# Low parts of weights by accumulating DMA instead of a subtraction on VectorE, in a two-layer decoder step

## The chip, the core and the metric

The kernel runs on one core of one Trainium2 chip. The metric is the device time of one execution, in microseconds (us). Two timed runs of the kernel before took 2398.39 and 2399.04 us, median 2398.72 us. One further execution was profiled; it took 2399.39 us, and its first and last instruction lie 2397.4 us apart (the span).

## The reference

The reference is one inference step of a small decoder with 512 prompt positions and 32 new tokens (8 sequences of 4), so 544 columns of activations, width 1024. Two layers follow each other, each a SwiGLU, a mixer and another SwiGLU:

```python
for i in range(DEPTH):                                        # DEPTH = 2
    xp = xp + 0.5 * swiglu(rmsnorm(xp, norm_ffn1[i]), w_ffn1_in[i], w_ffn1_out[i])
    hp = rmsnorm(xp, norm_mix[i])
    # even layer: dilated-window attention, q/k/v of 3 groups x 8 heads x 64, one output projection
    # odd layer:  chunked gated MLP, u, v = split(gelu(h W_uv)), v = layernorm(v), (u * (tril(W_s) v + b)) W_o
    xp = xp + mp
    xp = xp + 0.5 * swiglu(rmsnorm(xp, norm_ffn2[i]), w_ffn2_in[i], w_ffn2_out[i])

def swiglu(x, w_in, w_out):
    gate, up = jnp.split(x @ w_in, 2, axis=-1)                # 1024 -> 2 x 2816
    return (jax.nn.silu(gate) * up) @ w_out                   # 2816 -> 1024
```

The same is done for the 32 new tokens, with cached keys and values in the attention. Everything is float32: the weights come from HBM as float32, and the products have to hold that precision.

## The kernel before, in words

TensorE is fed 32-bit operands in a rounded format (F32R). To keep float32 precision, every operand is split into a high part (the value rounded) and a low part (the value less the high part), and each product is three matmuls: high weights times high activations, high weights times low activations, low weights times high activations (`passes`, one of each per 128 x 128 weight tile and 272 columns). A weight tile's parts are called `wh` and `wl`.

The work is a sequence of *mults*. Each takes one slab of raw weights, K feature tiles of 128 rows by 256 columns (K is 8, 6 or 2), that one DMA on SyncE's queue brings into one of three buffers `raw` (two during the attention). There are two ways to multiply:

- `plain` splits the slab into its two column halves (`split` once per half), and runs 4 output quarters x K tiles x 3 passes, which is 96 matmuls for K = 8 and 72 for K = 6. It serves the output projections, the attention's projections and the first gate of each feed-forward part.
- `seven` serves the other gate and up slabs and the gated MLP's u and v. It forms sums and differences of the slab's four quarters on VectorE (`s13`, `s24`) and does seven products in place of eight, 84 matmuls. It needs four splits: of the quarter `a11` (128 x 512), of `s13` and `s24` (128 x 1024), and last of the odd feature tiles of the slab as they are (128 x 1024), which give the weights of the products that `c11` and `c21` close.

`split` (lines 219 to 226) is one ScalarE copy that rounds into `wh`, and one VectorE subtraction that writes `wl`. Both go into one of `g.nw` = 4 pairs of buffers, so a split can start only when the matmuls that read the buffer's former content are through. The products land in PSUM banks; ScalarE copies three of a seven's out (`k1`, `k5`, `k6`), VectorE the others, and both also prepare the activations' high and low parts (`spread`).

The order on every engine is made by a scheduler when the program is built; it goes by its own estimate of how long each instruction takes, and interleaves the products of neighbouring mults on TensorE accordingly. Each engine then works off its list in that fixed order, whatever the times are on the chip. `g.soon()` raises the priority of a piece of work during the attention, while `g.few` is set.

GpSimd (POOL) has work only in the attention and, once, two multiplications and additions in the gated MLP.

Of the kernel before, what the change touches and what calls it, by code (L numbers as in the profile page):

```python
# [9 lines left out]
F32 = mybir.dt.float32  # L10
F32R = mybir.dt.float32r
AF = mybir.ActivationFunctionType
ALU = mybir.AluOpType
# [3 lines left out]
P = 128  # L17
D = 1024
KD = D // P
# [5 lines left out]
NEG = -1.0e30  # L25
RMS_EPS = 1e-6
LN_EPS = 1e-5
SCRATCH = 64
XC = 256

UNITS = "U0 AV' BV' b A0 K0 B0 U1 E0 rk0 K1 B1 U2 rk1 K2 A12 B2 U3 E12 rk2 M D v0 v1 U4 v2"
# [197 lines left out]
def split(g, a):  # L229

    k, n = a.shape[1:]
    t = [g.wp.tile([P, KD * P], F32R, tag=nm, name=nm, bufs=g.nw)[:, :k * n].rearrange("p (k n) -> p k n", k=k) for nm in ("wh", "wl")]
    g.nc.scalar.copy(t[0], a)  # L233
    add(g.nc.vector, t[1], a, t[0], ALU.subtract)
    return t
# [13 lines left out]


def load_raw(g, src, K, cols):
    raw = g.raw()[:, :K * cols].rearrange("p (k n) -> p k n", k=K)
    g.nc.sync.dma_start(raw, src.rearrange("(k p) n -> p k n", p=P))
    return raw


def plain(g, raw, K, x, ev, hook=None):

    ws = []
    for c in range(2):  # L260
        with g.soon():
            ws.append(split(g, raw[:, :K, c * P:(c + 1) * P]))
    w = lambda c, k: [v[:, k] for v in ws[c]]
    halves = [(c, h) for c in range(2) for h in range(2)]

    def take(c, h, z):
        with g.soon():
            ev.full(c, h, z)

    if hook is None:  # L270
        for c, h in halves:
            z = g.bank("z")[:, :H2]
            for k in range(K):
                passes(g, z, w(c, k), x.tile(k, h), k == 0, k == K - 1)
            take(c, h, z)
        return

    g.late()
    zs = [g.bank("z")[:, :H2] for _ in halves]
    for k in range(K - 2):  # L280
        for (c, h), z in zip(halves, zs):
            passes(g, z, w(c, k), x.tile(k, h), k == 0, False)
    hook()
    for (c, h), z in zip(halves, zs):
        for k in range(K - 2, K):
            passes(g, z, w(c, k), x.tile(k, h), False, k == K - 1)
        take(c, h, z)


def seven(g, raw, K, x, ev, hook=None):  # L290

    nc = g.nc
    n = K // 2
    rv = raw[:, :K].rearrange("p (k e) (i c) -> p e i k c", e=2, i=2)
    a11, a12, a21 = rv[:, 0, 0], rv[:, 1, 0], rv[:, 0, 1]
    a22 = rv[:, 1, 1]
    V = nc.vector
    s13, s24 = (g.wp.tile([P, 2, 4, P], F32, tag=f"s{i}", name=f"s{i}")[:, :, :n] for i in range(2))

    def parts(a):  # L300
        with g.soon():
            return split(g, a)

    def take(to, z):
        with g.soon():
            to(z)

    def both(s):
        v = parts(s.rearrange("p i k c -> p (i k) c"))
        return [u[:, :n] for u in v], [u[:, n:] for u in v]  # L310

    w1 = parts(a11)
    with g.soon():
        add(V, s13[:, 0], a21, a22, ALU.add)
        add(V, s13[:, 1], a11, a21, ALU.subtract)
    w5, w7 = both(s13)
    with g.soon():
        add(V, s24[:, 0], s13[:, 0], a11, ALU.subtract)
        add(V, s24[:, 1], a12, s24[:, 0], ALU.subtract)
    z1, z3, z2 = g.banks()  # L320
    product(g, z1, w1, x.b(B11), True, True)
    take(ev.p1, z1)
    product(g, z3, w5, x.t(T1), True, True)
    take(ev.p5, z3)
    w6, w3 = both(s24)
    product(g, z1, w6, x.t(T2), False, True)
    take(ev.p6, z1)
    product(g, z3, w3, x.b(B22), False, True)
    take(ev.c12, z3)
    v = parts(raw[:, :K].rearrange("p (k e) n -> p e k n", e=2)[:, 1])  # L330
    w2, w4 = ([u[:, :, i * P:(i + 1) * P] for u in v] for i in range(2))
    product(g, z1, w7, x.t(T3), False, True)
    take(ev.c22, z1)
    product(g, z2, w2, x.b(B21), True, True)
    take(ev.c11, z2)
    product(g, z1, w4, x.t(T4), False, True)
    take(ev.c21, z1)
# [360 lines left out]

def qkv_unit(g, w_qkv, units, dst, hook):

    raw = g.raw().rearrange("p (k n) -> p k n", k=KD)
    for e, (c, gi, hp) in enumerate(units):
        col = ((c * 3 + gi) * 8 + 2 * hp) * 64
        g.nc.sync.dma_start(raw[:, :, e * P:(e + 1) * P], w_qkv[:, col:col + P].rearrange("(k p) n -> p k n", p=P))
    mult(g, "qkv", raw, KD, g.xop, Rows(g, dst, [u[1] > 0 for u in units], hook is not None), hook)


# [469 lines left out]
def gmlp(g, xop, w_uv, ln_g, ln_b, w_s, b_s, w_out, v_out, nxt):  # L1177
    nc = g.nc
    vd = g.tc.nc.dram_tensor("v_rows", (T, DV), F32, kind="Internal").ap()
    with ExitStack() as stack:  # L1180
# [10 lines left out]
        def spatial():  # L1191
            wn = gp.tile([P, 4 * H2], F32, tag="abl1", name="wsn")[:, :8 * P].rearrange("p (k s) -> p k s", k=8)
            nc.scalar.dma_start(wn, w_s.rearrange("g t s -> t g s"))
            nc.vector.tensor_tensor(wn, wn, cst[:, C_TRIL - C_B:C_TRIL - C_B + 128].unsqueeze(1).to_broadcast([P, 8, P]), op=ALU.mult)
            for gq in range(2):
                ps = g.bank("sm")
                for k in range(4):
                    nc.tensor.transpose(ps[:, k * P:(k + 1) * P], wn[:, 4 * gq + k], g.ident)
                nc.vector.tensor_copy(wst[:, 4 * gq:4 * gq + 4], ps.rearrange("p (k t) -> p k t", k=4))
            ps = g.bank("sm")  # L1200
            ws4 = gp2.tile([4, 8, 4], F32, tag="ws4", name="ws4")
            nc.vector.tensor_copy(ws4, wst[:4, :, :4])
            nc.tensor.matmul(ps[:32, :32], cst[:4, C_REP - C_B:C_REP - C_B + 32], ws4.rearrange("p g t -> p (g t)"), start=True, stop=True)
            ws32 = gp2.tile([32, 8, 4], F32, tag="ws32", name="ws32")
            nc.vector.tensor_copy(ws32, ps[:32, :32].rearrange("p (g t) -> p g t", g=8))
            for k in range(8):
                nc.vector.tensor_tensor(wss[:, k], ws32[:, k].unsqueeze(1).to_broadcast([32, 8, 4]),
                                        cst[:32, C_BM - C_B:C_BM - C_B + 32].rearrange("p (b t) -> p b t", t=4), op=ALU.mult)
# [84 lines left out]
        def mixing(j, vn, vs):  # L1293

            for n in range(4):
                nc.scalar.activation(vn[:, n], vn[:, n], AF.Identity, bias=lt[:, n:n + 1], scale=lr[:, n:n + 1])
            nc.scalar.activation(vs, vs, AF.Identity, bias=lt[:32, 4:5], scale=lr[:32, 4:5])
            mix = g.pair()
            for i in range(2):
                gq = (j + i) // 3  # L1300
                iss = slice(i * P, (i + 1) * P)
                if gq not in rows:
                    rsb = gp2.tile([P, P], F32, tag="rsb", name="rsb")
                    bsb = gp2.tile([P, P], F32, tag="bsb", name="bsb")
                    nc.scalar.dma_start(bsb, b_s[gq:gq + 1].to_broadcast([P, P]))
                    pr = g.bank("sm")
                    nc.tensor.matmul(pr[:, :P], g.cst[:, C_ONES:C_ONES + 128], wst[:, gq], start=True, stop=True)
                    nc.scalar.activation(rsb, pr[:, :P], AF.Copy, scale=float(D))
                    rows[gq] = rsb, bsb
                pm = g.bank("sm")  # L1310
                for n in range(4):
                    nc.tensor.matmul(pm[:, n * P:(n + 1) * P], vn[:, n, iss], wst[:, gq], start=True, stop=True)  # L1312
                pn = g.bank("sm")
                nc.tensor.matmul(pn[:, :32], vs[:, iss], wss[:, gq].rearrange("p b t -> p (b t)"), start=True, stop=True)
                rsb, bsb = rows[gq]
                gc = g.gT[:, 48 + j + i:49 + j + i]
                bc = g.gT[:, 72 + j + i:73 + j + i]
                off = gp.tile([P, P], F32, tag="off", name="off")
                nc.vector.scalar_tensor_tensor(off, rsb, bc, bsb, op0=ALU.mult, op1=ALU.add)
                fo = mix[:, i]  # L1320
                nc.vector.scalar_tensor_tensor(
                    fo[:, :TP].rearrange("p (n t) -> p n t", n=4), pm.rearrange("p (n t) -> p n t", n=4), gc,
                    off.unsqueeze(1).to_broadcast([P, 4, P]), op0=ALU.mult, op1=ALU.add)
                nc.vector.scalar_tensor_tensor(
                    fo[:, TP:].rearrange("p (n t) -> p n t", n=8), pn[:, :32].rearrange("p (n t) -> p n t", n=8), gc,
                    off[:, :4].unsqueeze(1).to_broadcast([P, 8, 4]), op0=ALU.mult, op1=ALU.add)
            return mix
# [108 lines left out]
```

## Time and profile before

| what | value |
|---|---|
| median of two timed runs | 2398.72 us |
| profiled execution, its own time | 2399.39 us |
| span of its instructions | 2397.4 us |
| TensorE busy | 2345.2 us, 98% of the span |
| VectorE busy | 1807.4 us, 75% |
| ScalarE busy | 1127.2 us, 47% |
| POOL busy | 117.1 us, 5% |
| bytes moved by DMA | 261.45 MB, mean 109 GB/s |

Busy time is the time in which at least one instruction of the engine is under way, and the span is what all engines share. TensorE's 52.2 us outside its busy time are all that could be won by waiting less. The weight loads of TensorE (PEld) overlap its matmuls. The granted clock of TensorE was 0.991 over the span.

### The profile page before, as it was taken

The numbers are of one execution on the slowest core, as the hardware profiler recorded it, in microseconds if no ns is written. First come the engines' busy times: TensorE is split into PE (matmuls) and PEld (weight loads), VectorE is DVE, ScalarE is ACT, GpSimd is POOL, SyncE is SP. The second block draws the span as 40 slices with busy tenths as digits, with TensorE's granted clock in tenths as the row PEclk, the third lists the DMA queues.
The fourth block names the chain that finished last, engine by engine and source line by source line (L and its number), as shares of the span: only waits on it lengthen the run. The fifth ranks groups of instructions, "written<-read, shape, count | busy, mean of one in ns | idle before, by whom it ended". The sixth has DMA issues, their size and how long they took to land.

```text
span 2397.4 us, 44282 instructions
## 1 busy us (share of the span) xinstructions
PE 2345.2 (98%) x18380; PEld 2296.5 (96%) x18380; DVE 1807.4 (75%) x3059; ACT 1127.2 (47%) x1844; POOL 117.1 (5%) x102
## 2 busy tenths in 40 slices
PE   7999999999999899999999999999999999999997
PEld 6999999989988799999999999999999999999997
DVE  7878585657656887858786959789977768878583
ACT  5535254434434643525553525556744536435253
POOL 0000000224223000000000000000000000000000
PEclk9999999999999999999999999999999999999999
DMA  3323235546435232323222323344443222323231
GB/s 128 105 89 115 80 106 166 142 132 190 132 109 157 93 106 85 123 71 117 76 91 92 120 71 111 103 132 136 126 131 121 91 80 88 106 89 123 72 115 38
DMA packets 306529, 261.45 MB, mean 109 GB/s; under 512 B 7160, under 2 KB 302936, under 8 KB 306200
## 3 DMA queue, kind: packets, MB, share of 16 engines
q1 hardware_dynamic: 283016, 241.05, 32.0%
q10 hardware_dynamic: 23312, 17.57, 2.5%
q8 instruction: 144, 2.36, 0.4%
q14 instruction: 57, 0.47, 0.1%
HBM read 241.94 MB, written 16.65 MB: 108 GB/s over the span
## 4 chain that ended last, share of the span: by engine, by line
PE 92%; DVE 4%; DMA 1%; ACT 1%; issue 1%; POOL 0%; ACTq 0%; POOLq 0%; DVEq 0%
PE ps_z L242 85%; PE ps_sm L1312 1%; DVE wl L226 1%; DMA cache<-in_cache_kv_w_dram 1%; PE ps_sm L850 1%; DVE s L226 1%; PE ps_sm L819 1%; DMA other<-in_cache_kv_w_dram 0%; PE ps_sm L497 0%; PE ps_sm L1241 0%; DVE xbl L226 0%; DVE f L226 0%; PE ps_sb L1038 0%; DVE tl L226 0%; PE ps_sb L1167 0%
## 5 line engine op out<-in xcount | busy, mean ns | idle before, releaser
L242 PE MATMUL ps_z<-xbh,wh 128*128 128x272 f32 x2084 | 606.6, 294 | 14.6 <-DVE s L226 5.1
L233 ACT CAST wh<-raw 128x1024 fp32r<-128x1024 f32 (+3 forms) x404 | 353.5, 876 | 558.4 <-PE ps_z L242 531.3
L242 PE MATMUL ps_z<-xbl,wh 128*128 128x272 f32 x2084 | 604.7, 291 | 1.5 <-DVE xbl L781 1.1
L242 PE MATMUL ps_z<-xbh,wl 128*128 128x272 f32 x2084 | 601.7, 292 | 1.8 <-DVE wl L226 1.8
L242 PE MATMUL ps_z<-abh,wl 128*128 128x272 f32 x1792 | 515.9, 290 | 0.0
L242 PE MATMUL ps_z<-abl,wh 128*128 128x272 f32 x1792 | 513.7, 288 | 0.0
L242 PE MATMUL ps_z<-abh,wh 128*128 128x272 f32 x1792 | 513.3, 289 | 0.0
L242 PE MATMUL ps_z<-th,wl 128*128 128x272 f32 x1712 | 495.8, 290 | 0.7 <-DVE wl L226 0.7
L242 PE MATMUL ps_z<-th,wh 128*128 128x272 f32 x1712 | 495.3, 290 | 0.6 <-ACT k L352 0.3
L242 PE MATMUL ps_z<-tl,wh 128*128 128x272 f32 x1712 | 494.2, 289 | 0.0
L226 DVE TENSOR_TENSOR wl<-raw,wh 128x1024 fp32r<-128x1024 f32 (+3 forms) x404 | 413.8, 1027 | 55.0 <-ACT wh L233 51.6
L242 PEld LDWEIGHTS ps_z<-xbh,wh 128*128 128x128 f32 x2084 | 393.5, 190 | 22.7 <-DVE s L226 5.9
L242 PEld LDWEIGHTS ps_z<-xbl,wh 128*128 128x128 f32 x2084 | 395.5, 190 | 4.1 <-DVE xbl L781 1.7
L242 PEld LDWEIGHTS ps_z<-xbh,wl 128*128 128x128 f32 x2084 | 393.0, 189 | 5.4 <-DVE wl L226 2.7
L233 ACT CAST wh<-s 128x1024 fp32r<-128x1024 f32 x214 | 224.3, 1049 | 274.3 <-PE ps_z L242 269.3
L242 PEld LDWEIGHTS ps_z<-abl,wh 128*128 128x128 f32 x1792 | 337.5, 189 | 0.3
L242 PEld LDWEIGHTS ps_z<-abh,wl 128*128 128x128 f32 x1792 | 336.5, 188 | 0.2
L242 PEld LDWEIGHTS ps_z<-abh,wh 128*128 128x128 f32 x1792 | 335.4, 188 | 0.5
L242 PEld LDWEIGHTS ps_z<-th,wh 128*128 128x128 f32 x1712 | 323.5, 189 | 1.5 <-ACT k L352 0.8
L242 PEld LDWEIGHTS ps_z<-th,wl 128*128 128x128 f32 x1712 | 323.3, 189 | 1.3 <-DVE wl L226 1.1
L242 PEld LDWEIGHTS ps_z<-tl,wh 128*128 128x128 f32 x1712 | 323.5, 189 | 0.1
L226 DVE TENSOR_TENSOR wl<-s,wh 128x1024 fp32r<-128x1024 f32 x214 | 261.0, 1220 | 31.7 <-ACT wh L233 31.5
(268 smaller groups left out, 2470.8 us busy)
## 6 DMA issues: line engine op xcount, KB each, us to landing
raw<-in_w_ffn_in_dram SPq DMA_DIRECT2D x88, 1024.0 KB, 5.1
raw<-in_w_ffn_out_dram SPq DMA_DIRECT2D x32, 1024.0 KB, 5.2
raw<-in_w_uv_b_dram SPq DMA_DIRECT2D x24, 1024.0 KB, 5.3
raw<-in_w_qkv_a_dram SPq DMA_DIRECT2D x36, 512.0 KB, 5.4
other<-in_cache_kv_w_dram SPq DMA_DIRECT2D x28, 512.0 KB, 4.6
raw<-in_w_ffn_out_dram SPq DMA_DIRECT2D x16, 768.0 KB, 4.4
raw<-in_w_out_b_dram SPq DMA_DIRECT2D x16, 768.0 KB, 4.5
other<-in_cache_kv_w_dram SPq DMA_DIRECT2D x28, 256.0 KB, 4.7
```

What stands on the lines that cost most here:

```text
L226: eng.tensor_tensor(out, a, b, op=op)
L233: g.nc.scalar.copy(t[0], a)
L242: g.nc.tensor.matmul(z, a, b, start=(first and s == 0), stop=(last and s == 2), skip_group_check=True)
L819: nc.tensor.matmul(pe[e][:, n % 2, lo:], q0[es, n * P:(n + 1) * P], k0[es, n * P - P + lo:(n + 1) * P], start=True, stop=True)
L850: nc.tensor.matmul(pe[e][:, r % 2, 128 * gi - 128:128 * gi], tl["q", gi][es, rs], tl["k", gi][es, rs], start=True, stop=True)
L1312: nc.tensor.matmul(pm[:, n * P:(n + 1) * P], vn[:, n, iss], wst[:, gq], start=True, stop=True)
```

## The change

Outside the attention, a split of raw weights no longer takes a subtraction on VectorE. ScalarE writes the high part, then writes the negated high part into the low part's buffer, and a DMA issued from GpSimd adds the raw weights onto it (`split_half`). That is done for the last split of each `seven` and for both splits of each `plain`. The splits of `a11`, `s13` and `s24`, and all splits during the attention, stay as they were (`split`).

So that such a DMA has whole rows to move, the slab is laid out with its even feature tiles first and its odd ones behind them: two DMAs per slab, each of half the bytes. A `plain` then no longer splits by column half: its two splits are the even and the odd feature tiles, over all 256 columns.

The space for the descriptors of GpSimd's DMAs grows from 64 to 512 bytes per partition; some small buffers of the gated MLP are single or shared instead, to make room.

```diff
-SCRATCH = 64
+SCRATCH = 512
...
 def load_raw(g, src, K, cols):
-    raw = g.raw()[:, :K * cols].rearrange("p (k n) -> p k n", k=K)
-    g.nc.sync.dma_start(raw, src.rearrange("(k p) n -> p k n", p=P))
+    raw = halves_of(g.raw()[:, :K * cols], K)
+    for e in range(2):
+        g.nc.sync.dma_start(raw[:, e], src.rearrange("(k e p) n -> e p k n", p=P, e=2)[e])
     return raw
...
+def halves_of(raw, K):
+    return raw.rearrange("p (e k n) -> p e k n", e=2, k=K // 2)
+
+def split_half(g, a):
+    k = a.shape[1]
+    if g.few:
+        return split(g, a)
+    t = [g.wp.tile([P, KD * P], F32R, tag=nm, name=nm, bufs=g.nw)[:, :k * 256].rearrange("p (k n) -> p k n", k=k) for nm in ("wh", "wl")]
+    g.nc.scalar.copy(t[0], a)
+    g.nc.scalar.activation(t[1], t[0], AF.Copy, scale=-1.0)
+    g.nc.gpsimd.dma_start(t[1], a, accum_op=ALU.add)
+    return t
...
 def plain(g, raw, K, x, ev, hook=None):
     ws = []
-    for c in range(2):
+    for e in range(2):
         with g.soon():
-            ws.append(split(g, raw[:, :K, c * P:(c + 1) * P]))
-    w = lambda c, k: [v[:, k] for v in ws[c]]
+            ws.append(split_half(g, raw[:, e]))
+    w = lambda c, k: [v[:, k // 2, c * P:(c + 1) * P] for v in ws[k % 2]]
...
 def seven(g, raw, K, x, ev, hook=None):
-    rv = raw[:, :K].rearrange("p (k e) (i c) -> p e i k c", e=2, i=2)
+    rv = raw.rearrange("p e k (i c) -> p e i k c", i=2)
...
-    v = parts(raw[:, :K].rearrange("p (k e) n -> p e k n", e=2)[:, 1])
+    with g.soon():
+        v = split_half(g, raw[:, 1])
     w2, w4 = ([u[:, :, i * P:(i + 1) * P] for u in v] for i in range(2))
...
-            ws4 = gp2.tile([4, 8, 4], F32, tag="ws4", name="ws4")
+            ws4 = gp.tile([4, 8, 4], F32, tag="ws4", name="ws4")
...
-                off = gp.tile([P, P], F32, tag="off", name="off")
+                off = g.ssum[:, :P]
```

The change also moves instructions, since the scheduler makes its order anew. In the whole program 255 subtractions leave VectorE's list, 255 copies are added to ScalarE's and 255 DMAs to POOL's: 181 of 128 x 1024 elements, 64 of 128 x 768 and 8 of 128 x 256, besides two at the very start.

**ScalarE's list in the first feed-forward part.** Before, in the third slab of the second chunk (`raw_1797`): `wh` are high parts, `s0` and `s1` the sums of quarters, `k1` and `k5` products that leave PSUM.

```order
L233 CAST wh_1807<-s0_1799 128x1024 [waits PE_49,Activation_49]
L233 CAST wh_1844<-s1_1800 128x1024 [waits DVE_49,PE_49]
L233 CAST wh_1875<-raw_1797 128x1024 [waits PE_49,Activation_49]
L352 COPY k1_1828<-ps_z_1813 128x272 [waits DVE_49,PE_49]
L356 COPY k5_1842<-ps_z_1814 128x272 [waits DVE_49,PE_49]
L233 CAST wh_1927<-raw_1923 128x512 [waits DMAHW1_49,PE_49]
```

In the changed kernel, the same slab is `raw_1828`:

```order
L233 CAST wh_1876<-s1_1832 128x1024 [waits DVE_49,PE_49]
L371 COPY k1_1860<-ps_z_1845 128x272 [waits DVE_49,PE_49]
L269 CAST wh_1907<-raw_1828 128x1024 [waits DMAHW6_49,PE_49]
L270 ACTIVATE wl_1908<-wh_1907 128x1024 [waits DMASW4_49,PE_49,Activation_49]
L375 COPY k5_1874<-ps_z_1846 128x272 [waits DVE_49,PE_49]
L379 COPY k6_1892<-ps_z_1845 128x272 [waits PE_49]
L233 CAST wh_1961<-raw_1956 128x512 [waits DMAHW7_49,PE_49]
```

The negated copy `wl_1908` stands right behind the high part `wh_1907`, and `k1` has moved ahead of both.

**TensorE's list where that slab's last split is first needed.** Before, the first matmul that reads `wl_1876` waits for VectorE (DVE):

```order
L242 MATMUL ps_z_1939<-xbh0_74,wh_1927 128x272 [waits Activation_49]
L242 MATMUL ps_z_1939<-xbl0_78,wh_1927 128x272
L242 MATMUL ps_z2_1815<-xbh0_74,wl_1876 128x272 [waits DVE_49]
L242 MATMUL ps_z2_1815<-xbh1_75,wh_1875 128x272
L242 MATMUL ps_z2_1815<-xbl1_79,wh_1875 128x272
```

Now the first matmul that reads `wl_1908` waits for a DMA of GpSimd (the semaphore DMASW2):

```order
L242 MATMUL ps_z_1845<-th3_289,wl_1840 128x272
L242 MATMUL ps_z_1973<-xbh0_74,wh_1961 128x272 [waits Activation_49]
L242 MATMUL ps_z_1973<-xbl0_78,wh_1961 128x272
L242 MATMUL ps_z2_1847<-xbh0_74,wl_1908 128x272 [waits DMASW2_49]
L242 MATMUL ps_z2_1847<-xbh1_75,wh_1907 128x272
L242 MATMUL ps_z2_1847<-xbl1_79,wh_1907 128x272
```

The place is the same; the wait is for another source. The buffer of `wl_1908` held `wl_1712` before, whose last reader stands 63 matmuls ahead of this row.

**TensorE's list where a `plain` follows a `seven`.** Before, at the first output projection of the second chunk (`raw_2552`, output banks 2562 and 2588), only the first column half `wh_2554`, `wl_2555` is read here; the second, `wh_2558`, is first read 72 rows below this piece's first:

```order
L242 MATMUL ps_z_2562<-abh0_1536,wh_2554 128x272 [waits Activation_49]
L242 MATMUL ps_z_2562<-abl0_1540,wh_2554 128x272
L242 MATMUL ps_z_2588<-abh0_1536,wh_2554 128x272 [waits DVE_49]
L242 MATMUL ps_z_2588<-abl0_1540,wh_2554 128x272
L242 MATMUL ps_z_2562<-abh0_1536,wl_2555 128x272 [waits DVE_49]
L242 MATMUL ps_z_2562<-abh0_1536,wh_2554 128x272
```

Now the even tiles (`wh_2598`, `wl_2599`) and the odd ones (`wh_2603`, `wl_2604`) are read in turn from the start:

```order
L242 MATMUL ps_z_2608<-abh0_1563,wl_2599 128x272 [waits DMASW0_49]
L242 MATMUL ps_z_2608<-abh0_1563,wh_2603 128x272 [waits Activation_49]
L242 MATMUL ps_z_2608<-abl0_1567,wh_2603 128x272
L242 MATMUL ps_z_2634<-abh0_1563,wl_2599 128x272
L242 MATMUL ps_z_2634<-abh0_1563,wh_2603 128x272
L242 MATMUL ps_z_2634<-abl0_1567,wh_2603 128x272
L242 MATMUL ps_z_2660<-abh0_1563,wl_2599 128x272
L242 MATMUL ps_z_2660<-abh0_1563,wh_2603 128x272
```

The scheduler has put matmuls on high parts of several output banks ahead of the first one that needs `wl_2604`, which comes 14 rows below this piece's first and 55 matmuls after the last reader of its buffer's former content.

More of the change, by code (lines that the diff above doesn't have):

```diff
@@ L699, in qkv_unit @@
 def qkv_unit(g, w_qkv, units, dst, hook):
-    raw = g.raw().rearrange("p (k n) -> p k n", k=KD)
-    for e, (c, gi, hp) in enumerate(units):
+    raw = halves_of(g.raw(), KD)
+    for i, (c, gi, hp) in enumerate(units):
         col = ((c * 3 + gi) * 8 + 2 * hp) * 64
-        g.nc.sync.dma_start(raw[:, :, e * P:(e + 1) * P], w_qkv[:, col:col + P].rearrange("(k p) n -> p k n", p=P))
+        for e in range(2):
+            g.nc.sync.dma_start(raw[:, e, :, i * P:(i + 1) * P], w_qkv[:, col:col + P].rearrange("(k e p) n -> e p k n", p=P, e=2)[e])
     mult(g, "qkv", raw, KD, g.xop, Rows(g, dst, [u[1] > 0 for u in units], hook is not None), hook)
@@ L1200, in spatial @@
             ps = g.bank("sm")
-            ws4 = gp2.tile([4, 8, 4], F32, tag="ws4", name="ws4")
+            ws4 = gp.tile([4, 8, 4], F32, tag="ws4", name="ws4")
             nc.vector.tensor_copy(ws4, wst[:4, :, :4])
             nc.tensor.matmul(ps[:32, :32], cst[:4, C_REP - C_B:C_REP - C_B + 32], ws4.rearrange("p g t -> p (g t)"), start=True, stop=True)
-            ws32 = gp2.tile([32, 8, 4], F32, tag="ws32", name="ws32")
+            ws32 = gp.tile([32, 8, 4], F32, tag="ws32", name="ws32")
             nc.vector.tensor_copy(ws32, ps[:32, :32].rearrange("p (g t) -> p g t", g=8))
```

## The prediction

> **What bounds the kernel now.** I read the page's first part, then the chain of waits, then busy time by stretches of 60 us, then who TensorE (PE) waits for.
>
> ```profile
> span 2397.4 us, 44282 instructions
> PE 2345.2 (98%) x18380; PEld 2296.5 (96%) x18380; DVE 1807.4 (75%) x3059; ACT 1127.2 (47%) x1844; POOL 117.1 (5%) x102
> PE 92%; DVE 4%; DMA 1%; ACT 1%; issue 1%; POOL 0%; ACTq 0%; POOLq 0%; DVEq 0%
> ...
> 0.00:60.00 60.00, 46.92 (x259) 40.51 (x260) 47.27 (x82) 34.92 (x50) 0.20 (x4) 0.94 0.40 128
> 60.00:120.00 60.00, 60.00 (x480) 60.00 (x479) 52.71 (x79) 30.45 (x41) 0.00 (x0) 1.00 0.33 106
> ...
> 720.00:780.00 60.00, 55.06 (x407) 48.77 (x407) 40.67 (x94) 26.59 (x73) 22.85 (x22) 0.91 0.52 154
> 780.00:840.00 60.00, 48.70 (x338) 45.85 (x337) 53.16 (x95) 37.25 (x57) 0.00 (x0) 0.94 0.31 98
> ...
> 2340.00:2400.00 60.00, 42.08 (x339) 41.44 (x337) 22.30 (x67) 22.06 (x88) 0.00 (x0) 0.89 0.10 38
> ...
> PE ps_z L242 <- DVE s L226: 5.1, 3, 4.6
> PE ps_z L242 <- ACT wh L233: 4.7, 4, 1.7
> ...
> PE ps_z L242 <- DVE wl L226: 2.5, 3, 1.4
> ```
>
> The columns of a stretch are its length, the busy time (and count) of PE, PEld, DVE, ACT and POOL, the clock, the DMA engines' busy share, GB/s. In a full stretch PE does 480 matmuls in 60.00 us: 0.125 us each, with no gap. Of the 52.2 us in which PE is not busy (2397.4 - 2345.2), 13.1 lie in the first 60 us, 16.2 between 720 and 840 us where the attention ends, and 15.3 after 2340 us (57.4 - 42.1): 44.6 us at the program's start, the attention's end and the last stores. Some 8 us are left for all the rest. So DVE at 75% is nowhere the bound; the chain has it at 4%.
>
> **The change, part by part.**
>
> *Removed: 255 subtractions on DVE. Added: 255 negating copies on ACT.*
>
> ```profile
> L233 ACT CAST wh<-raw 128x1024 fp32r<-128x1024 f32 x217 | 227.8, 1050 | 293.4 <-PE ps_z L242 274.7 <-issue 18.5
> L233 ACT CAST wh<-raw 128x768 fp32r<-128x768 f32 x64 | 53.0, 833 | 120.7 <-PE ps_z L242 112.4 <-issue 5.3 <-DVE wl L226 2.9
> L575 ACT ACTIVATE s<-s 128x1088 f32<-128x1088 f32 x44 | 49.0, 1113 | 3.9 <-DVE s L226 3.9
> ...
> L226 DVE TENSOR_TENSOR wl<-raw,wh 128x1024 fp32r<-128x1024 f32 x217 | 274.0, 1263 | 35.7 <-ACT wh L233 35.3
> L226 DVE TENSOR_TENSOR wl<-raw,wh 128x768 fp32r<-128x768 f32 x64 | 60.9, 954 | 11.7 <-ACT wh L233 11.5
> ```
>
> 183 x 1.263 + 64 x 0.954, with the eight small ones, is some 295 us less on DVE (75% to 63%). The negating copy isn't in the trace; an ACTIVATE of 128x1088 took 1.11 us, so 128x1024 takes 1.05, as the CAST does. 183 x 1.05 + 64 x 0.83 + 3 is some 250 us more on ACT (47% to 57%). Both lie beside PE. What they are worth on the path: PE's waits for DVE's `wl` are 2.5 us in all, of which the splits that stay keep a share. I book 0 for the relief, at most the 8 us above.
>
> *The new chain to a low part.* Before, a buffer that comes free is filled by one CAST and one subtraction. These rows show the hand-overs:
>
> ```profile
> 1002.18 1.05 ACT L233 CAST wh<-raw 128x1024 fp32r<-128x1024 f32 x1 [0.97 <-PE ps_z L242]
> ...
> 1003.27 1.23 DVE L226 TENSOR_TENSOR wl<-raw,wh 128x1024 fp32r<-128x1024 f32 x1 [0.50 <-ACT wh L233]
> ...
> 1010.24 0.29 PE L242 MATMUL ps_z<-th,wl 128*128 128x272 f32 x1
> ...
> 1010.50 1.05 ACT L233 CAST wh<-raw 128x1024 fp32r<-128x1024 f32 x1 [3.54 <-PE ps_z L242]
> ```
>
> From the start of the last matmul that reads the old content to the CAST are 0.26 us (1010.24 to 1010.50), from the CAST's end to the subtraction 0.04 (1003.23 to 1003.27). The chain before is 0.26 + 1.05 + 0.04 + 1.23 = 2.6 us. The new one is 0.26 + 1.05 + 1.05 + two hand-overs of 0.05 + D = 2.46 + D, where D is the time from the accumulating DMA's release to its landing. PE is full, so each time that this chain is longer than what PE has to do between the two matmuls, PE loses the difference, and nothing gives it back.
>
> *What PE has to do in between* is counted in the order: matmuls from the last reader of a buffer's old low part to the first reader of the new, at 0.125 us each. For the 181 accumulations of 128x1024 (the two at the very start have nothing ahead): 4 have 27 to 46 matmuls; 13 have 55 (a `plain` behind a `seven`, the third place shown above); 4 have 59 to 61; 45 have 63, 7.9 us (the second place, the run of a `seven` behind a `seven`); 12 have 65; the others 67 or more. Of the 64 of 128x768, 9 have 50 to 55, of the 8 small ones 4 have 27 to 33.
>
> *D.* No GpSimd DMA and no SBUF-to-SBUF one is in the trace. The nearest rows:
>
> ```profile
> raw<-in_w_ffn_in_dram SPq DMA_DIRECT2D x88, 1024.0 KB, 5.1
> raw<-in_w_qkv_a_dram SPq DMA_DIRECT2D x36, 512.0 KB, 5.4
> raw<-in_w_ffn_out_dram SPq DMA_DIRECT2D x16, 768.0 KB, 4.4
> vr<-v_rows ACTq DMA_DIRECT2D x12, 512.0 KB, 3.7
> out_dram<-xf SPq DMA_DIRECT2D x4, 512.0 KB, 3.6
> xs<-in_x_sample_dram ACTq DMA_DIRECT2D x1, 128.0 KB, 2.5
> ...
> L226 POOL TENSOR_TENSOR prod<-other,sc x64: 612/882/1508, 480.4 to 764.2; 128x512 f32<-128x512 f32 x32, 128x256 f32<-128x256 f32 x32
> ```
>
> An accumulation of 128x1024 writes 512 KB and must read 1024 (the raw weights and what stands there). If only the 512 KB counted, D would be 3.7; if reading and writing came after each other, 5.1 + 3.6 = 8.7. The nearest row is that which reads 1024 KB, 5.1, and POOL has to issue it; POOL's shortest piece of work in this trace took 0.61 us. I take D = 5.1 + 0.6 = 5.7, for 768 columns 4.4 + 0.6 = 5.0, for 256 columns 2.5 + 0.6 = 3.1.
>
> The Trainium skill says in *Collectives: The Full Stack*, "The bandwidth ceiling: the fold count and why AG ≠ RS ≠ AR", that an add in the DMA engines is slower "because the add needs two source reads", by nearly a factor of two; no transfer of this trace adds. In *DMA: Bandwidth & Descriptors*, "Anatomy of one DMA — SWDGE (gpsimd) path", it gives 2.0 us and bytes at 436 GB/s, which would be an estimate of 4.4 us for 1 MB, where this trace has 5.1 for a load of that size: the measurement decides, and the page is on the short side.
>
> *The sum at D = 5.7*: a chain of 8.16 us, or 65.3 matmuls.
> - 4 with 27, 39, 45 and 46: short by 38.3 + 26.3 + 20.3 + 19.3 = 104 matmuls, 13.0 us
> - 13 with 55: short by 10.3 each, 16.7 us
> - 4 with 59 to 61: 2.5 us
> - 45 with 63: 2.3 each, 12.9 us
> - 12 with 65: 0.4 us
> - 128x768: 0.26 + 2 x 0.83 + 0.1 + 5.0 = 7.0 us, 56 matmuls; those with 50, 51, 53 (three) and 55 (four) lose 24, 3 us
> - the small ones: 2 us.
>
> Together 50 us. The slope is what matters: the same sum gives 21 us at D = 5.1, 28 at 5.4, 85 at 6.0, 120 at 6.3, 210 at 7.0 and some 500 at 8.7, since ever more of the list falls short. (From 5.7 up it includes 24 of the 128x1024 whose copy stands behind a `k1` that waits for a product, with 62 matmuls behind that product.)
>
> *Raw weights in two DMAs.* 0.37 us of SP for each more issue; SP is not waited for. Three buffers are loaded ahead; a slab's loads wait for its accumulation instead of DVE's subtraction, which costs some 5 us of a lead of more than a mult (84 x 0.125 = 10.5 us). Nothing, while that cover lasts. The loads start when an accumulation lands and take 5.1 us; the next accumulation is released 10.5 - 7.9 + 2.5 = 5.1 us later. They just miss each other; where they meet, D grows, which is in the range.
>
> *POOL's two multiplications and additions in the gated MLP* (1.9 us each) now stand ahead of an accumulation. In ACT's list that one's negated copy comes 19 rows behind the row on which these two wait, so they are done by then: 0.
>
> *Even and odd splits during the attention*: both halves are needed at once, where the second came half a mult later. They still take 2.6 us and have 104 matmuls (13 us) or more for 128x1024: 0.
>
> Sum: 2399.4 + 50 = 2449, say **2450 us**. That sum stands on the profiled execution's own time, 2399.39, 0.03% above the median of the runs.
>
> **The rivals.**
> 1. *The DMA is quick and everything fits* (D up to 5.4). For it: the rows at 3.6 and 3.7 for 512 KB. Against it: twice the bytes read, the issue through POOL. The sum runs from 5 to 28 us; with some relief on DVE, 2398 to 2427, about 2410: no slower than before that can be told. It decides at D = 5.65, where the sum reaches 47 us.
> 2. *The DMA is slow, or shares the engines with the loads* (D above 6.3). For it: 512 KB loads that run beside others took 5.4, as long as 1024 KB alone, so sharing costs 1.7; a `plain` issues two accumulations in a row. 5.7 + 1.3 gives D = 7 and 2399 + 210 = 2610; at 8.7 it would be 2900.
> 3. *Faster: DVE's and ACT's lists loosen and PE's gaps close.* 48 us of 52.2 would have to go; 44.6 of them lie at the start, the attention's end and the last stores. At best 2390.
>
> That the change doesn't do what it says is excluded by the lists: the subtractions are gone, the DMAs are there, and PE waits for them.
>
> **How the numbers follow.** Forecast, D between 5.4 and 6.3, 2427 to 2520: 0.38. Rival 1: 0.36. Rival 2: 0.22. Rival 3 by over 2%: 0.02. Slower for another cause: 0.02. A measurement of this kernel tells about 2% from no change, 48 us. Of the forecast's 0.38 some 0.12 lie below 2447. Slower: 0.26 + 0.22 + 0.02 = 0.50; same: 0.36 + 0.12 = 0.48; faster: 0.02. The range leaves out a tenth at each end: from 2398 (the quickest DMA with the relief) to 2610 (rival 2 at D = 7). The forecast's own range is 2427 to 2520.
>
> **What would show it.** A row for `wl` from `raw` on POOL's queue with 255 issues, 5.7 us to landing for 512 KB; PE waiting for that DMA in `ps_z`, some 80 times, 0.3 us in the runs of `seven`, 1.3 us where a `plain` begins, in all about 50 us; no PE wait for it between 380 and 760 us; ACT near 1380 us and DVE near 1515 us busy. A landing under 5.4 us, or PE gaps that name ACT or a PSUM bank instead, would prove the forecast wrong; so would a landing that is right while PE waits little, since then the count of matmuls is not what PE has in hand.

## The result and the profile after

The changed kernel took 2700.72 us (two timed runs, 2691.58 and 2709.86) against 2398.72 us before: a ratio of 1.126, with an interval from 1.110 to 1.142. It is slower by 302 us, where 50 us were forecast and the range ended at 2610. The profiled execution took 2709.86 us.

The page's first part, and the row of GpSimd's own DMA queue (packets, MB, share of 16 engines' span):

```profile
span 2708.1 us, 45349 instructions
PE 2444.1 (90%) x18380; PEld 2369.1 (87%) x18380; DVE 1562.0 (58%) x2804; ACT 1346.2 (50%) x2099; POOL 342.4 (13%) x357
...
q0 software_dynamic: 36720, 122.18, 23.8%
```

VectorE (DVE) and ScalarE (ACT) did what the change asked: DVE lost 245 us, ACT won 219. TensorE (PE) does the same 18380 matmuls, but its span is 310.7 us longer. That splits in two: its idle time rose from 52.2 to 264.0 us (2708.1 - 2444.1), 211.8 more, and its busy time rose by 98.9 us. The waits name who it idles for (us in total, times, longest):

```profile
POOL wl L271 <- issue: 378.4, 63, 9.8
...
PE ps_z L242 <- DMA wl<-raw: 209.1, 106, 6.1
```

209.1 us of PE's 264.0 idle us are waits for the accumulating DMA, which is nearly all that was added. The page says in its costliest groups in which products (the last columns are the idle time ahead of the group and what ended it), and in its DMA part how long the DMA took from issue to landing (median us, the last column):

```profile
L242 PE MATMUL ps_z<-abh,wl 128*128 128x272 f32 x1792 | 548.2, 310 | 168.3 <-DMA wl<-raw 168.1
L242 PE MATMUL ps_z<-xbh,wl 128*128 128x272 f32 x2084 | 600.8, 296 | 41.0 <-DMA wl<-raw 41.0
...
wl<-raw POOLq DMA_DIRECT2D x183, 512.0 KB, 4.7
wl<-raw POOLq DMA_DIRECT2D x64, 384.0 KB, 4.5
```

`abh` are the activations of the output projections, which are all `plain`. Four fifths of the waiting is theirs. The median accumulation isn't slow: 4.7 us for 512 KB is a microsecond *less* than I took. But the medians hide two groups. Over all accumulations the time to landing is

```profile
DMA to landing us min/median/max: 2.7/4.7/10.4
```

Of the `plain`'s 148, counted from the DMA packets in the trace, 41 of 512 KB and 34 of 384 KB had no load of raw weights beside them (under 50 KB moved by SyncE's queue) and took 4.5 and 3.9 us in the median. 35 and 29 had one beside them (over 300 KB) and took 8.3 and 7.0. Busy time by stretches of 60 us shows the alternation of waits (columns as before):

```profile
120.00:180.00 60.00, 52.34 (x383) 51.68 (x382) 23.07 (x41) 17.78 (x25) 6.09 (x7) 0.93 0.56 137
180.00:240.00 60.00, 60.00 (x481) 60.00 (x480) 51.60 (x79) 39.58 (x52) 4.39 (x5) 1.00 0.55 145
240.00:300.00 60.00, 50.74 (x378) 49.32 (x377) 16.26 (x29) 20.30 (x23) 7.86 (x9) 0.94 0.67 158
300.00:360.00 60.00, 60.00 (x481) 60.00 (x480) 42.63 (x66) 32.57 (x44) 4.37 (x5) 1.00 0.50 132
```

The stretches from 180 and from 300 us are runs of `seven` behind `seven`, and PE is as full as before (481 matmuls). The stretches from 120 and from 240 us, which hold runs of `plain` behind `plain`, lose a fifth of the matmuls and show a lower clock.

So accumulations make PE wait in the one kind of mult and not in the other. What differs is that a `plain` issues two in a row. POOL's timeline through the first output projection (start, duration, engine, line, in brackets the idle time before and what ended it):

```profile
114.55 0.88 POOL L271 DMA_DIRECT2D wl<-raw  x1 [6.16 <-ACT wl L270]
118.81 0.87 POOL L271 DMA_DIRECT2D wl<-raw  x1 [3.38 <-issue]
125.93 0.88 POOL L271 DMA_DIRECT2D wl<-raw  x1 [6.25 <-issue]
130.20 0.87 POOL L271 DMA_DIRECT2D wl<-raw  x1 [3.39 <-ACT wl L270]
138.68 0.88 POOL L271 DMA_DIRECT2D wl<-raw  x1 [7.61 <-issue]
142.94 0.87 POOL L271 DMA_DIRECT2D wl<-raw  x1 [3.39 <-issue]
```

On ACT, in the same stretch, the negated copy of one of these halves:

```profile
112.81 0.83 ACT L270 ACTIVATE wl<-wh 128x768 fp32r<-128x768 f32 x1
```

And on PE the waits for accumulations:

```profile
118.54 0.59 PE L242 MATMUL ps_z<-abh,wl 128*128 128x272 f32 x1 [1.39 <-DMA wl<-raw]
...
129.93 0.39 PE L242 MATMUL ps_z<-abh,wl 128*128 128x272 f32 x1 [2.45 <-DMA wl<-raw]
...
142.67 0.60 PE L242 MATMUL ps_z<-abh,wl 128*128 128x272 f32 x1 [3.41 <-DMA wl<-raw]
```

This projection has four `plain`, so four pairs. The first pair left POOL at 107.52 and 114.55; the others are 118.81 with 125.93, 130.20 with 138.68, and 142.94 with 151.23. The second of a pair never starts right behind the first, nor the next pair right behind the second. PE sees an accumulation land at 118.54, 129.93 and 142.67, and POOL takes up the next at 118.81, 130.20 and 142.94: 0.27 us later, three times out of three. The negated copy that ACT finished at 113.64 (112.81 + 0.83) gets its accumulation only at 125.93, 12.3 us later. POOL's row often names nothing that it waits for ("issue"). Over the whole trace, 114 of the `plain`'s 148 accumulations are held back like this: they leave POOL more than 0.7 us after their negated copy is done (the others 0.4 us), and each of them leaves 0.26 to 0.32 us after the one before it has landed. Two are never under way at once. Of the `seven`'s 107 none is held back.

The landing at 118.54 also ends the use of a slab, and SyncE (SP) loads the next one into its place:

```profile
118.61 0.90 SPq L255 DMA_DIRECT2D raw<-in_w_ffn_out_dram  x2
```

The accumulation that leaves POOL at 118.81 runs beside these loads, the one at 125.93 doesn't (line 271, from 118.6 to 120 us and from 125.7 to 127):

```profile
DMA to landing us min/median/max: 6.8/6.8/6.8
...
DMA to landing us min/median/max: 4.0/4.0/4.0
```

In this stretch a pair occupies POOL's queue for 11.4 us (118.81 to 130.20) and for 12.7 us (130.20 to 142.94), while such a `plain` gives PE 72 matmuls, 9.0 us. That is a queue that runs slower than PE.

### The profile page after: what moved, and what is told of

It reads as the page before. It is cut to its first block, busy times and chain, and to the rows that moved or that the text cites. A ratio compares the mean times of both kernels' runs of the same rounds, so it can differ in the third digit from the quotient of the medians.

```text
span 2708.1 us, 45349 instructions
## 1 busy us (share of the span) xinstructions
PE 2444.1 (90%) x18380; PEld 2369.1 (87%) x18380; DVE 1562.0 (58%) x2804; ACT 1346.2 (50%) x2099; POOL 342.4 (13%) x357
## 5 line engine op out<-in xcount | busy, mean ns | idle before, releaser
L242 PE MATMUL ps_z<-abh,wl 128*128 128x272 f32 x1792 | 548.2, 310 | 168.3 <-DMA wl<-raw 168.1
L242 PE MATMUL ps_z<-abh,wh 128*128 128x272 f32 x1792 | 541.1, 303 | 0.4 <-DVE x L408 0.4
L242 PE MATMUL ps_z<-abl,wh 128*128 128x272 f32 x1792 | 539.5, 302 | 0.0
L242 PEld LDWEIGHTS ps_z<-abh,wl 128*128 128x128 f32 x1792 | 361.0, 203 | 186.5 <-DMA wl<-raw 186.3
L271 POOL DMA_DIRECT2D wl<-raw x255 | 223.1, 875 | 2064.8 <-ACT k L375 665.8
L269 ACT CAST wh<-raw 128x1024 fp32r<-128x1024 f32 (+2 forms) x255 | 244.2, 972 | 383.4 <-PE ps_z L242 377.3
L408 DVE SCALAR_TENSOR_TENSOR x<-ps_z,x 128x272 f32<-128x272 f32 x288 | 123.4, 438 | 463.6 <-PE ps_z L242 460.8
L242 PEld LDWEIGHTS ps_z<-abh,wh 128*128 128x128 f32 x1792 | 364.6, 204 | 0.8 <-DVE x L408 0.7
L242 PEld LDWEIGHTS ps_z<-abl,wh 128*128 128x128 f32 x1792 | 364.0, 203 | 0.2
```

The source lines that it names most:

```text
L242: g.nc.tensor.matmul(z, a, b, start=(first and s == 0), stop=(last and s == 2), skip_group_check=True)
L271: g.nc.gpsimd.dma_start(t[1], a, accum_op=ALU.add)
L408: self.g.nc.vector.scalar_tensor_tensor(v, z, self.scale, v, op0=ALU.mult, op1=ALU.add)
```

## The experiments

The theory that the expectations call A: with 512 bytes of descriptor space per partition POOL can hold one accumulation of this size, and holds the second back until the first has landed. Its rivals are that the space has nothing to do with it (B), and that each accumulation costs for itself, in a `seven` as in a `plain`, and their number counts (C). The kernels are edits of the changed one. Each time is set against runs of the kernel before beside it, medians 2399.51 us for the first four kernels and 2399.84 for the others, seven runs each. The edited kernels were run four times, `copy_dma` twice.

### More space for descriptors: `room768` and `room896`

```diff
-SCRATCH = 512
+SCRATCH = 768        # room768;  896 in room896
```

The order on every engine is that of the changed kernel.

> The changed kernel with 768 instead of 512 bytes per partition for the descriptors of GpSimd's DMAs; the order of every engine is the same. Theory A (room): at 512 bytes POOL can hold one accumulation of this size and issues the next only when the former has landed, so the pairs of a plain leave POOL 4.3 to 8.7 us apart. With half as much room again a second one fits: the two of a pair leave POOL about 1 us apart, TensorE's wait for wl falls from 209 us to under 80, and the time is 2430 to 2520 us. Theory B (engines): the accumulations of a pair are slow because they share the DMA engines with each other and with the loads; then more room changes nothing: 2680 to 2720 us, or each of a pair lands later than now.

> The same with 896 bytes. Theory A: if the room for descriptors counts in steps of one accumulation, a third one fits and POOL never holds one back in a plain: 2400 to 2460 us, not slower than with 768. Theory B: no change against 512, 2680 to 2720 us.

Measured: 2531.51 us with 768 bytes (ratio 1.056, 1.054 to 1.058), 2517.97 us with 896 (1.050, 1.048 to 1.052). The waits of `room768`:

```profile
PE ps_z L242 <- DMA wl<-raw: 85.0, 53, 4.5
POOL wl L271 <- issue: 43.9, 16, 5.3
```

the landing, from its page:

```profile
wl<-raw POOLq DMA_DIRECT2D x64, 384.0 KB, 6.2
```

and POOL's timeline, two pairs of the same output projection:

```profile
126.45 1.76 POOL L271 DMA_DIRECT2D wl<-raw  x2 [9.31 <-PE ps_z L242]
135.52 1.77 POOL L271 DMA_DIRECT2D wl<-raw  x2 [7.30 <-ACT wl L270]
```

Of `room896` the waits:

```profile
PE ps_z L242 <- DMA wl<-raw: 77.2, 51, 4.7
```

and POOL's timeline, a little earlier than above:

```profile
107.64 0.86 POOL L271 DMA_DIRECT2D wl<-raw  x1 [4.09 <-ACT wl L270]
109.84 1.78 POOL L271 DMA_DIRECT2D wl<-raw  x2 [1.34 <-PE ps_z L242]
```

One number, which changes neither a transfer nor the order of anything, takes back 169 of the 302 us. With 768 bytes POOL sends both accumulations of a pair in one go (x2, 1.76 us), 9.1 us from pair to pair, which is PE's own 9.0 us; the row of waits that named nothing falls from 378.4 to 43.9 us. That refutes B and carries A, though 2531.51 us and 85.0 us of waits lie a little above the 2520 and 80 that A allowed. The gain stops there: with 896 bytes a third accumulation goes out within 4 us of the first (107.64, then two from 109.84), and only 14 us more are won, against the 2400 to 2460 that I expected. There is little left to hold back: 30 accumulations with 768 bytes, 5 with 896, by the count above. But two under way slow each other. With no load beside it, an accumulation of 384 KB that overlaps another one takes 6.0 us with 768 bytes (the median of 14), where it took 3.9 alone; the page's median over all is 6.2 (6.3 with 896). Of the 123.6 us by which the span of `room896` (2521.0) is longer than before, 77.2 are waits for accumulations and 42.5 are PE's longer busy time (2387.7).

### One kind of mult alone: `seven_only` and `plain_only`

```diff
 # seven_only, in plain
-            ws.append(split_half(g, raw[:, e]))
+            ws.append(split(g, raw[:, e]))
 # plain_only, in seven
-        v = split_half(g, raw[:, 1])
+        v = split(g, raw[:, 1])
```

> Accumulating DMAs only for the last split of each seven (107); both splits of a plain are by ScalarE and VectorE again, with the new layout. Theory A: one accumulation per 10.5 us always finds room, lands in 4.7 us and is in time: no wait for wl on a DMA worth more than 10 us, 2395 to 2420 us. Theory C (the chain of the prediction): each of them is late by the 0.3 us and more that the prediction worked out for a landing of 5.7 us: 2420 to 2440 us.

> Accumulating DMAs only for the two splits of each plain (148); the last split of a seven is by VectorE. Theory A: the loss is all here, since the pairs wait for each other on POOL: 2650 to 2710 us, TensorE waits 180 to 210 us for wl. Theory C: the loss is shared by all accumulations and this kernel keeps a part of it, 2500 to 2600 us.

Measured: 2425.89 us (1.012, 1.010 to 1.013) with the 107 accumulations of the `seven` alone, 2614.05 us (1.092, 1.088 to 1.095) with the 148 of the `plain` alone. The waits of `seven_only`:

```profile
PE ps_z L242 <- DMA wl<-raw: 22.4, 16, 6.4
```

of `plain_only`:

```profile
PE ps_z L242 <- DMA wl<-raw: 146.0, 69, 5.9
```

and two issues of POOL's timeline in `plain_only`, the second of one pair and the first of the next, again one landing apart:

```profile
118.66 0.89 POOL L271 DMA_DIRECT2D wl<-raw  x1 [6.33 <-issue]
122.88 0.87 POOL L271 DMA_DIRECT2D wl<-raw  x1 [3.33 <-issue]
```

The `plain` carry the loss: 214.5 us against 26.4, for 148 accumulations against 107. C would have both alike for each accumulation (1.45 and 0.25 us). But neither result is where A put it: `seven_only` should have lost nothing to speak of (2395 to 2420), and `plain_only` should have lost more (2650 to 2710). In `seven_only` the first wait of all comes at 823 us, behind the attention, and is the longest with 6.4 us; the rest are ten of 12.2 us behind 1500 us and a few in between. The two excesses add up to 240.9 us, 61 us short of the changed kernel's. No accumulation of a `seven` is held back in either kernel, but the `plain`'s stand longer in POOL's queue when both kinds are there: 114 of them for 760 us in all in the changed kernel, 107 for 534 us in `plain_only`. How much of the 61 us that makes is not shown.

### One accumulation per `plain`: `half_plain`

```diff
-            ws.append(split_half(g, raw[:, e]))
+            ws.append((split_half if e else split)(g, raw[:, e]))
```

The even half's low part comes from DVE again, the odd half's by accumulation, 512 bytes as in the changed kernel.

> As the changed kernel, but in a plain only the odd half's low part comes by accumulating DMA, the even half's by VectorE: one accumulation per mult everywhere, 512 bytes of room. Theory A (room): with one accumulation per 9 to 12 us POOL never has to hold one back, and most of the loss is gone: 2425 to 2480 us, TensorE waits under 60 us for DMA. Theory C (the chain from a freed buffer to a landed low part is too long for a plain even alone): waits of 100 us and more stay, 2550 to 2620 us.

Measured: 2490.81 us (1.038, 1.036 to 1.039). The waits:

```profile
PE ps_z L242 <- DMA wl<-raw: 66.8, 37, 6.9
```

Taking away 74 of the 255 accumulations, one of each pair, takes away 210 of the 302 us. So two of a pair cost far more than two lone ones. It is 11 us over what A allowed (and 66.8 us of waits are more than its 60), and far from C's band. 9 accumulations are still held back. The other waits are spread over the program, 15.8 us of them between 800 and 860 us alone; that there the chain is longer than the work in hand is likely, and not shown.

### Plain copies instead of accumulations: `copy_dma`

```diff
-    g.nc.gpsimd.dma_start(t[1], a, accum_op=ALU.add)
+    g.nc.gpsimd.dma_start(t[1], a)
```

The addition is left out, so the low parts hold the raw weights; the same bytes are written by as many DMAs in the same order.

> The changed kernel with the same 255 DMAs as plain copies of the raw weights instead of additions (the low parts are then wrong in value; nothing else is left out); the order of every engine is the same. Theory A (room): a copy has half as much to read and so half as many descriptors on the reading side, so more than one fits in 512 bytes; the pairs leave POOL about 1 us apart and the time is 2430 to 2530 us, no more than with 896 bytes. Rival G (any GpSimd DMA waits until the one before has landed): the pairs stay 4 us and more apart, 2600 to 2700 us. A landing of 512 KB that falls from 4.7 us to 3.7 or less says that the second reading is what it is made of; one that stays above 4.3 says that it isn't.

Measured: 2429.43 us (1.012, 1.010 to 1.014). The waits:

```profile
PE ps_z L242 <- DMA wl<-raw: 21.7, 18, 2.5
```

the landing, from the page:

```profile
wl<-raw POOLq DMA_DIRECT2D x183, 512.0 KB, 3.2
wl<-raw POOLq DMA_DIRECT2D x64, 384.0 KB, 3.4
```

and POOL's timeline, one pair of an output projection:

```profile
118.18 0.53 POOL L271 DMA_DIRECT2D wl<-raw  x1 [7.61 <-PE ps_z L242]
118.91 0.53 POOL L271 DMA_DIRECT2D wl<-raw  x1 [0.21 <-issue]
```

With 512 bytes, two copies leave POOL 0.73 us apart: the space holds two copies where it doesn't hold two accumulations, which read a second source for each row they write. Three things differ with it: 4.7 against 3.2 us to landing, 0.87 against 0.53 us of POOL, and the space. The run changes all three at once, so it doesn't share the 271 us that it saves out among them; `room768` gives the part of the space alone.

The Trainium skill says in *Collectives: The Full Stack*, "The bandwidth ceiling: the fold count and why AG ≠ RS ≠ AR", that an add in the DMA engines is slower for its two source reads, by nearly a factor of two. Here the factor is 1.5 (4.7 over 3.2) for a whole DMA from issue to landing.

### The layout alone, and the best of both: `layout_only` and `seven896`

`layout_only` makes both edits of the one-kind kernels, so that all low parts come from DVE and only the two loads per slab, the even and odd splits, the descriptor space and the shared small buffers are left of the change. `seven896` is `seven_only` with 896 bytes.

```diff
 # seven896
-SCRATCH = 512
+SCRATCH = 896
-            ws.append(split_half(g, raw[:, e]))
+            ws.append(split(g, raw[:, e]))
```

> No accumulating DMA at all: every split by ScalarE and VectorE, but even and odd feature tiles loaded apart and plain split by them. Theory A: the layout costs next to nothing, 2395 to 2410 us, and the 26 us by which the kernel with accumulations in the sevens alone is slower are those accumulations'. Rival L (layout): the odd half of a plain is needed at once, so the layout itself costs the 26 us: 2415 to 2430 us.

> Accumulating DMAs only for the last split of each seven, with 896 bytes of room. Theory A: where only one accumulation comes per 10.5 us room is never short, so this is the same as with 512 bytes, 2420 to 2432 us, and the 22 us of waits there come from the chain. Rival: those waits are also for room, 2400 to 2412 us.

Measured: `layout_only` 2403.36 us (1.001, 1.000 to 1.003), `seven896` 2422.67 us (1.010, 1.008 to 1.012). The busy times of `layout_only`:

```profile
PE 2346.6 (98%) x18380; PEld 2298.8 (96%) x18380; DVE 1805.6 (75%) x3059; ACT 1120.1 (47%) x1844; POOL 118.9 (5%) x102
```

PE's busy time in `layout_only` is that of the kernel before within 1.4 us. The two half loads and the even and odd split cost nothing that can be told. And where no pairs are issued, more space wins nothing that can be told either (2420.41 to 2427.98 against 2422.50 to 2432.17): the space matters for pairs alone. No version with accumulations beats the kernel before.

## Why the prediction was wrong

- **What bounds the kernel: right.** DVE at 75% was not the bound. `layout_only` has DVE back at 1805.6 us and is as quick as the kernel before, and no kernel with less work on DVE was quicker. Nothing contradicts the 0 booked for the relief, though no run has the relief alone. DVE came to 1562.0 us and ACT to 1346.2, where some 1515 and 1380 stood.
- **D, the time to landing: too long for the `seven`, too short for nearly half of the `plain`.** 5.7, 5.0 and 3.1 us were taken; 4.7, 4.5 and 2.7 are the medians. The estimate of 4.4 us for 1 MB, which the prediction took from the Trainium skill (*DMA: Bandwidth & Descriptors*, "Anatomy of one DMA — SWDGE (gpsimd) path") and set aside as short, was the nearer one for an accumulation of 512 KB with no load beside it, 4.5 us. At 4.7 the chain to a low part is 2.46 + 4.7 = 7.16 us, 57 matmuls, and the list of gaps gives 9.0 us for the four shortest, 3.7 for the 13 with 55 and some 2 for the rest: rival 1's case. With that one D for all, the sum would have lost about 15 us, which can't be told from no change.
- **The count of matmuls in hand: right for the runs of `seven`.** The 45 with 63 matmuls should not wait at D = 4.7, and between 160 and 245 us PE doesn't wait once for an accumulation. A landing under 5.4 us was named as what would prove the forecast wrong, and it did.
- **The step that failed: each accumulation was costed by itself, with D from its own release.** POOL's share in it was set at 0.6 us, as if the queue took the second of a pair right behind the first. So the pairs of a `plain`, with 72 and 96 matmuls in which to fetch both, fell out of the sum as harmless. In fact 114 of the `plain`'s 148 wait out the one before them, and a pair of 384 KB occupies the queue for 11.4 to 12.7 us where PE has 9.0 us of work. `room768` (169 us back with the space alone), `half_plain` (210 us back with one of each pair gone) and `plain_only` (214.5 of the 302 us) show it.
- **Loads and accumulations meet.** The prediction had them just miss each other, by the timing of a run of `seven`. In a run of `plain`, one landing lets SP load (118.61) and POOL send the accumulation that it held back (118.81), and the landings beside loads took 8.3 and 7.0 us where 5.7 and 5.0 stood. This is read from the trace; no run takes the loads away. Rival 2 named both parts, "shares the engines with the loads" and "a `plain` issues two accumulations in a row", but as a longer D for all, 7 us and 2610 us. What it lacked is the queue, on which these times add up.
- **PE's waits: 106 of 209.1 us,** against some 80 of 50 us, four fifths of them in the output projections.
- **A second term that stood nowhere: PE's busy time, +98.9 us.** The sum took every lost microsecond as a wait and every matmul at 0.125 us. Behind a long wait they run slower (last section). Matmuls that start 0.18 to 0.26 us behind the one before, with no idle time between, are 1311 against 606 before; what they take over 0.125 us each makes 72 of the 98.9 us.
- **The small terms held.** Two loads per slab, even and odd splits: 0, by `layout_only`. No accumulation keeps PE waiting between 450 and 820 us, where the attention does its splits on DVE. But five waits, 11.5 us in all, lie between 380 and 450 us, where the prediction had none.

What stays open: the last 118 us of `room896`, where next to nothing is held back, are not shared out between later landings, ACT's place in the chain and PE's slower matmuls.

## What to carry to other kernels

A DMA queue can hold back a DMA whose inputs are ready, and then a DMA's time to landing counts once for each one ahead of it. Cost a stage that issues two in a row by the time both take on the queue, against the work that the stage gives the bound engine, and look at what one landing sets off at the same moment: here the loads that slowed the next accumulation. A median to landing can hide two groups, so look at the smallest and the largest too. Where the issuing engine idles with no wait named and each issue follows a landing by a constant 0.3 us, look at the descriptor space first; an accumulating DMA took more of it here than a copy of the same bytes. In this kernel PE was full, so work taken off DVE won nothing, and the waits put in its place cost more than their length.

## What the runs showed of the hardware that was not expected

**Descriptor space decides how many accumulations are under way.** For accumulations of 384 and 512 KB, the most under way at once in the whole trace are one with 512 bytes per partition (issues 4.26 us apart at the least in the stretch shown), two with 768 (1.76 us for both) and three with 896; copies of the same bytes go 0.73 us apart with 512.

**Loads beside an accumulation nearly double its time.** 4.5 us alone and 8.3 beside loads for 512 KB, 3.9 and 7.0 for 384 KB (medians, changed kernel; the smallest beside loads are 5.3 and 4.9, the largest alone 6.0 and 6.5).

**Matmuls are slower after a long wait.** In the changed kernel's PE timeline, behind the wait of 2.45 us and behind that of 3.41 us:

```profile
130.54 0.29 PE L242 MATMUL ps_z<-abh,wh 128*128 128x272 f32 x1
130.66 0.28 PE L242 MATMUL ps_z<-abl,wh 128*128 128x272 f32 x1
...
143.07 0.43 PE L242 MATMUL ps_z<-abh,wh 128*128 128x272 f32 x1
143.29 0.43 PE L242 MATMUL ps_z<-abl,wh 128*128 128x272 f32 x1
143.52 0.43 PE L242 MATMUL ps_z<-abh,wl 128*128 128x272 f32 x1
```

The first two start 0.12 us apart, the others 0.23, and so on until about 145.8 us, when the pace is 0.12 again. Of the 15 waits of PE from 3.5 us up in this trace (counted from 60 us on, whatever ended them), 13 had such a run (seven matmuls and more) at once behind them, and the other two a few matmuls later; of the 32 waits between 2 and 3.5 us, 12 at once; of the 39 between 1 and 2 us, 6, and at five of these the pace was already slow before the wait. Most of these runs are 11 to 25 matmuls long and cost 1 to 2.5 us on top of the wait, and the granted clock of the stretch from 120 us is 0.93. The Trainium skill has it in *TensorE: Matmul & The Clock Gate*, "Part 1: The HAM clock gate": half the clock after an idle window of about 3.4 us that runs freely, and some 3.4 us of work until it is whole again. The trace agrees on the half rate and on the length of a slow run, about 3 us for most; but waits of 2 to 3.5 us already bring it on, 12 times out of 32.
